# One weight tile per gate: how the gate columns of a projection reach TensorE

## The chip, the cores and the metric

The kernel runs on one core of a Trainium2 chip. The metric is the time of one execution on the device, in microseconds. Before the change three executions took 1739.06, 1737.99 and 1738.39 us; the median is 1738.39 us.

## The reference, cut to what matters

The program is a decoder trunk of two layers over 512 tokens of width 1024. In each layer one projection of the normalised input `u` feeds three attention mixers and three gates:

```
z = u @ w_in                      # 7240 columns; the last 3 * 1024 are the gates
o_a, o_b, o_c = sparse attention, dilated attention, windowed attention with sinks
g = sigmoid(gates.reshape(B, L, 3, 1024))
merged = g[:, :, 0] * (o_a @ w_a) + g[:, :, 1] * (o_b @ w_b) + g[:, :, 2] * (o_c @ w_c)
h = h + merged @ w_o
h = h + relu(rmsnorm(h) @ w_up)^2 @ w_down
```

All of it is float32. The gates of one layer are a product of (512 x 1024) by (1024 x 3072).

## The kernel before, in words

**Products in three parts.** A float32 operand is split into a high part (rounded to the engine's float32r format) and a low part (what is left). `mm3` (lines 285 to 290) multiplies high by high, high by low and low by high, three matmuls into one PSUM tile. The activations `uT` stay split in SBUF for the whole layer. Weights are split as they arrive: `load` (lines 256 to 266) takes a `raw` tile of 128 partitions by 1024 columns, issues the DMAs into it on SP's queue (L261), casts it on ScalarE to `hi` (L264) and subtracts on VectorE to get `lo` (L265). The pool holds 6 `raw` tiles, 5 `hi` tiles and 5 `lo` tiles, and nearly every weight of the program passes through these rings (the MLP's `split`, L925 and L926, takes its `hi` and `lo` tiles from them too). A new tile is cast only when the oldest `hi` tile has been read for the last time.

**A gates chunk.** The 1024 gate columns are cut into eight chunks `f` of 128 columns. `gates` (lines 854 to 869) loads the weights of chunk `f` for all three gates with `load_chunk` (lines 268 to 283). That makes four tiles; tile j holds rows 256j to 256j + 255 of the weight matrix (two blocks of 128 rows, the contraction's `k` = 2j and 2j + 1) for 3 x 128 columns, so it is 768 columns wide and comes by three DMAs of 128 KB. The product of each gate then runs over k = 0..7, 24 matmuls of 512 columns, and so goes through all four tiles; the tiles come free one after another while the third gate is computed. Each gate ends with a tanh on ScalarE (L865) that is stored to DRAM, to be used by `branches` later. `gates` is a generator that yields after k = 3 and after each gate, six times for a chunk.

**What runs beside it.** `build` (from line 1147) draws steps of the gates in turn with steps of the attention mixers, two chunks beside each: chunks 0 and 1 beside `c_attend`, 2 and 3 beside the first `b_attend`, 4 and 5 beside the second, 6 and 7 beside `a_attend`, each time in both layers. Ahead of each of these lies a projection (`c_project`, `b_project`, `a_project`) whose own chunk is four tiles of the same rings. The steps of `topk` (L509, L510, VectorE only) are drawn with both `b_attend`s. The order of instructions on each engine in this part of the program is made when the program is built, by a list scheduler that goes by the order of the drawing and by when operands and buffers are expected to be ready; on the chip each engine runs its list strictly in order.

**Other lines that the prediction names.** L321, L322 and L325 are the rotary embedding of a projection's result on VectorE, L337 the transpose of it on TensorE, L682 the split of keys and queries on VectorE. L381 and L745 are the first steps of a softmax on VectorE, L386 and L750 its exponentials on ScalarE. L406 and L407 split the transposed probabilities, L757 and L561 are those transposes. L849 and L850 split the mixers' outputs for `branches`, whose weights pass through `load` as well.

Of the kernel before, what the change touches and what calls it, by code (L numbers as in the profile page):

```python
# [22 lines left out]
P = 128  # L23
T = 512
NT = 4
D = 1024
NK = 8
# [11 lines left out]
OFF_G = 4168  # L39
# [4 lines left out]
class Trunk:  # L44
# [808 lines left out]

    def gates(self, uT, w, f, sgs):
        nc = self.nc
        wk = self.load_chunk(w, 0, NK, [(OFF_G + i * D + f * P, P) for i in range(3)])
        for i in range(3):
            ps = self.psum([P, T], "g")
            for k in range(NK):
                lhs = tuple(x[:, i * P : (i + 1) * P] for x in wk[k])  # L860
                self.mm3(ps, lhs, (uT["hi"][:, k, :], uT["lo"][:, k, :]), k == 0, k == NK - 1)
                if k == 3:
                    yield
            sg = self.st([P, T], "t")
            nc.scalar.activation(sg, ps, AF.Tanh, scale=0.5)  # L865
            d = self.dr.tile([P, T], F32, name=self.uid("sgd"))
            nc.sync.dma_start(d, sg)
            sgs.append(d)
            yield
# [433 lines left out]
```

## Time and profile before

| | |
|---|---|
| median of 3 executions | 1738.39 us |
| profiled execution, own time | 1737.1 us |
| its span (first to last instruction) | 1735.4 us |
| TensorE (PE) busy | 1688.8 us, 97% |
| weight loads on TensorE (PEld) | 1429.2 us, 82% |
| VectorE (DVE) busy | 1304.6 us, 75% |
| ScalarE (ACT) busy | 919.4 us, 53% |
| mean granted TensorE clock | 0.997 |

How to read it: matmuls are pipelined, and each shows a duration longer than its distance to the next one, so a busy PE can still hide short gaps. Idle time of an engine counts only where something on the chain that ends last waits for it. A row of the chain of waits is a piece of that chain: the engine and line that the end of the program hung on at that time.

### The profile page before, as it was taken

The page shows a single profiled execution, that of the slowest core. Times are in us where ns is not written, and L with a number is a line of the kernel's source. Part 1 is how long each engine was busy: PE and PEld are TensorE (multiplying, and loading weights), DVE is VectorE, ACT ScalarE, POOL GpSimd, SP SyncE. Part 2 cuts the span into 40 slices and gives each one's busy share as a digit, 9 for nine tenths or more (in the row PEclk, how much of TensorE's full clock was granted, in tenths as well). Part 3 has the DMA queues.
Part 4 walks back from the last instruction along what each step waited for, and adds up shares of the span by engine and source line. Part 5 has one row for each costly group of instructions (what it writes and reads, how often), then busy time and mean ns, then how long its engine had stood idle before and what let it go on. Part 6 is the DMA issues. An engine that isn't in the chain of part 4 may idle for free.

```text
span 1735.4 us, 24490 instructions
## 1 busy us (share of the span) xinstructions
PE 1688.8 (97%) x8640; PEld 1429.2 (82%) x8640; DVE 1304.6 (75%) x2643; ACT 919.4 (53%) x1861; POOL 25.7 (1%) x80
## 2 busy tenths in 40 slices
PE   6999999999999999999999999999999999999997
PEld 4879889787789888888887898988778898888886
DVE  7886976968864858685888868597789568585868
ACT  5475655546533645454545855455473255455454
POOL 1100000000000000000000000000000000000000
PEclk9999999999999999999999999999999999999999
DMA  5333334332662142423343253433238423241411
GB/s 166 89 92 114 84 90 109 104 78 83 221 211 91 62 144 85 136 90 105 101 128 73 68 133 87 109 77 98 75 109 275 161 85 110 85 133 61 156 40 72
DMA packets 202908, 190.54 MB, mean 110 GB/s; under 512 B 17824, under 2 KB 159136, under 8 KB 202784
## 3 DMA queue, kind: packets, MB, share of 16 engines
q1 hardware_dynamic: 202784, 188.97, 36.6%
q8 instruction: 68, 1.11, 0.3%
q14 instruction: 56, 0.46, 0.1%
HBM read 167.91 MB, written 18.87 MB: 108 GB/s over the span
## 4 chain that ended last, share of the span: by engine, by line
PE 81%; DVE 12%; ACT 4%; issue 2%; DMA 1%; POOL 0%; SPq 0%; DVEq 0%; POOLq 0%; ACTq 0%
PE psg L288 20%; PE psg L289 20%; PE psg L290 20%; PE psl L289 2%; PE psl L290 2%; PE psl L288 2%; PE pst L337 2%; PE pst L289 1%; PE pst L290 1%; PE pst L288 1%; DVE a L682 1%; DVE lo L265 1%; PE psl L369 1%; PE pst L561 1%; PE psl L370 1%
## 5 line engine op out<-in xcount | busy, mean ns | idle before, releaser
L288 PE MATMUL psg<-uT,hi 128*128 128x512 f32 (+1 forms) x896 | 347.2, 387 | 0.0
L289 PE MATMUL psg<-uT,hi 128*128 128x512 f32 (+1 forms) x896 | 345.9, 386 | 0.0
L290 PE MATMUL psg<-uT,lo 128*128 128x512 f32 (+1 forms) x896 | 344.1, 384 | 0.0
L265 DVE TENSOR_TENSOR lo<-raw,hi 128x768 fp32r<-128x768 f32 (+4 forms) x256 | 262.8, 1031 | 56.3 <-ACT hi L264 54.0
L264 ACT CAST hi<-raw 128x768 fp32r<-128x768 f32 (+4 forms) x256 | 229.6, 900 | 129.8 <-PE psg L289 48.4
L288 PE MATMUL psg<-hi,uT 128*128 128x384 f32 (+2 forms) x624 | 220.9, 355 | 1.4 <-DVE t L322 1.4
L290 PE MATMUL psg<-hi,uT 128*128 128x384 f32 (+2 forms) x624 | 219.0, 352 | 0.6 <-DVE uT L241 0.6
L289 PE MATMUL psg<-lo,uT 128*128 128x384 f32 (+2 forms) x624 | 219.1, 352 | 0.1
L290 PEld LDWEIGHTS psg<-uT,lo 128*128 128x128 f32 x896 | 169.1, 189 | 31.7 <-DVE lo L265 0.9
L288 PEld LDWEIGHTS psg<-uT,hi 128*128 128x128 f32 x896 | 169.2, 189 | 30.2 <-issue 1.5
L289 PEld LDWEIGHTS psg<-uT,hi 128*128 128x128 f32 x896 | 169.2, 189 | 28.8
L925 ACT CAST hi<-raw 128x1024 fp32r<-128x1024 f32 x80 | 84.2, 1052 | 81.4 <-DVE raw L1000 34.6
L288 PEld LDWEIGHTS psg<-hi,uT 128*128 128x128 f32 x624 | 118.3, 190 | 8.4 <-issue 1.6
L289 PEld LDWEIGHTS psg<-lo,uT 128*128 128x128 f32 x624 | 118.1, 189 | 8.2 <-DVE lo L265 1.5
L290 PEld LDWEIGHTS psg<-hi,uT 128*128 128x128 f32 x624 | 118.0, 189 | 7.7 <-DVE uT L241 1.3
L926 DVE TENSOR_TENSOR lo<-raw,hi 128x1024 fp32r<-128x1024 f32 x80 | 96.0, 1218 | 25.4 <-ACT hi L925 25.4
L956 DVE TENSOR_TENSOR a<-t,a 128x512 fp32r<-128x512 f32 (+1 forms) x128 | 78.9, 620 | 46.9 <-ACT a L955 45.3
L288 PE MATMUL psg<-hi,a 128*128 128x512 f32 x288 | 112.5, 390 | 0.0
L290 PE MATMUL psg<-hi,a 128*128 128x512 f32 x288 | 112.2, 389 | 0.0
L289 PE MATMUL psg<-lo,a 128*128 128x512 f32 x288 | 112.0, 389 | 0.0
L964 ACT ACTIVATE t<-psg 128x512 f32<-128x512 f32 x60 | 35.7, 595 | 120.4 <-PE psg L290 120.4
L407 DVE TENSOR_TENSOR a<-pst,a 128x384 fp32r<-128x384 f32 (+1 forms) x100 | 60.5, 622 | 36.8 <-ACT a L406 36.3
(229 smaller groups left out, 3232.0 us busy)
## 6 DMA issues: line engine op xcount, KB each, us to landing
raw<-in_w_in_dram SPq DMA_DIRECT2D x336, 128.0 KB, 2.8
raw<-in_w_up_dram SPq DMA_DIRECT2D x128, 256.0 KB, 3.7
raw<-in_w_down_dram SPq DMA_DIRECT2D x48, 512.0 KB, 4.7
raw<-in_w_in_dram SPq DMA_DIRECT2D x24, 512.0 KB, 3.6
sgd<-t SPq DMA_DIRECT2D x48, 256.0 KB, 2.2
t<-sgd SPq DMA_DIRECT2D x48, 256.0 KB, 4.3
raw<-in_w_o_dram SPq DMA_DIRECT2D x16, 512.0 KB, 4.4
a<-in_w_down_dram SPq DMA_DIRECT2D x16, 512.0 KB, 4.3
```

Source lines behind the costliest of these rows:

```text
L264: nc.scalar.copy(hi[:, :width], raw[:, :width])
L265: nc.vector.tensor_tensor(lo[:, :width], raw[:, :width], f32(hi[:, :width]), op=ALU.subtract)
L288: nc.tensor.matmul(out, lh, rh, start=start, stop=False, **kw)
L289: nc.tensor.matmul(out, lh, rl, start=False, stop=False, **kw)
L290: nc.tensor.matmul(out, ll, rh, start=False, stop=stop, **kw)
L337: self.nc.tensor.transpose(ps[:, i, :], src[:, i * P : (i + 1) * P], self.ident)
L369: nc.tensor.matmul(out, q, k[:, 0, c0 : c0 + n], start=True, stop=False)
L407: self.last_dve = nc.vector.tensor_tensor(pt[:, 1, :n], ps, f32(pt[:, 0, :n]), op=ALU.subtract)
L925: nc.scalar.copy(hi, x)
L926: nc.vector.tensor_tensor(lo, x, f32(hi), op=ALU.subtract)
L956: v.tensor_tensor(lo, x, f32(hi), op=ALU.subtract)
L964: nc.scalar.activation(r, ps, AF.Relu)
```

## The change

A chunk is loaded as three tiles, one for each gate, with all eight blocks of 128 rows side by side: 1024 columns wide, one DMA of 512 KB. The matmul of gate i and block k takes its 128 columns from tile i at place k. The split of a tile is the same `load` as before: cast on ScalarE, subtraction on VectorE. The products, their order and the yields stay.

```
     def gates(self, uT, w, f, sgs):
         nc = self.nc
-        wk = self.load_chunk(w, 0, NK, [(OFF_G + i * D + f * P, P) for i in range(3)])
+        wk = []
+        for i in range(3):
+            c0 = OFF_G + i * D + f * P
+            src = w[:, c0 : c0 + P].rearrange("(k p) n -> p k n", p=P)
+            wk.append(self.load([(lambda raw: raw.rearrange("p (k n) -> p k n", n=P), src)], D))
         for i in range(3):
             ps = self.psum([P, T], "g")
             for k in range(NK):
-                lhs = tuple(x[:, i * P : (i + 1) * P] for x in wk[k])
+                lhs = tuple(x[:, k * P : (k + 1) * P] for x in wk[i])
                 self.mm3(ps, lhs, (uT["hi"][:, k, :], uT["lo"][:, k, :]), k == 0, k == NK - 1)
                 if k == 3:
                     yield
```

## Rows read from the trace of the kernel before

**Rows 1.** The page: busy time by engine; chain that ended last, by engine.
```profile
PE 1688.8 (97%) x8640; PEld 1429.2 (82%) x8640; DVE 1304.6 (75%) x2643; ACT 919.4 (53%) x1861; POOL 25.7 (1%) x80
...
PE 81%; DVE 12%; ACT 4%; issue 2%; DMA 1%; POOL 0%; SPq 0%; DVEq 0%; POOLq 0%; ACTq 0%
```

**Rows 2.** Chain of waits over the whole span, shares by line.
```profile
by line: PE psg L288 20.2%; PE psg L289 20.2%; PE psg L290 20.1%; issue 2.0%; PE psl L289 1.9%; PE psl L290 1.9%; PE psl L288 1.9%; PE pst L337 1.7%; PE pst L289 1.4%; PE pst L290 1.4%; PE pst L288 1.3%; DVE a L682 1.2%; DVE lo L265 1.2%; P
```

**Rows 3.** Waits of TensorE, in total: us, times, longest us.
```profile
PEld psl L369 <- DVE st L381: 6.8, 14, 1.0
...
PEld psg L289 <- DVE lo L265: 1.5, 5, 0.6
...
PEld psg L290 <- DVE lo L265: 0.9, 4, 0.2
...
PE pst L337 <- DVE t L325: 9.2, 14, 1.3
```

**Rows 4.** Groups by shape: count, busy us, mean ns, idle before and releasers.
```profile
L265 DVE TENSOR_TENSOR lo<-raw,hi 128x1024 fp32r<-128x1024 f32 x104 | 126.4, 1220 | 47.4 <-ACT hi L264 46.8
L265 DVE TENSOR_TENSOR lo<-raw,hi 128x768 fp32r<-128x768 f32 x112 | 105.9, 948 | 7.6 <-ACT hi L264 6.1 <-PE psg L290 0.5
L264 ACT CAST hi<-raw 128x1024 fp32r<-128x1024 f32 x104 | 109.3, 1051 | 74.5 <-PE psl L290 28.2 <-DMA raw<-in_w_up_dram 13.6 <-PE psg L289 12.0
L264 ACT CAST hi<-raw 128x768 fp32r<-128x768 f32 x112 | 93.0, 836 | 18.8 <-PE psg L289 8.0 <-PE psg L290 7.4 <-ACT a L672 2.3
```

**Rows 5.** Stretches: length, busy us of each engine (instructions), granted clock, DMA.
```profile
100.00:103.60 3.60, 2.36 (x13) 1.67 (x13) 3.54 (x19) 2.72 (x11) 0.00 (x0) 1.00 0.45 105
103.70:107.10 3.40, 3.40 (x10) 2.61 (x9) 2.16 (x13) 2.85 (x13) 0.00 (x0) 0.51 0.21 77
949.00:956.00 7.00, 5.71 (x33) 4.61 (x32) 6.76 (x24) 3.45 (x13) 0.00 (x0) 1.00 0.32 92
204.00:220.00 16.00, 14.33 (x82) 11.46 (x81) 14.63 (x45) 8.18 (x23) 0.00 (x0) 1.00 0.49 115
309.00:332.00 23.00, 19.73 (x115) 15.15 (x113) 22.47 (x58) 10.07 (x30) 0.00 (x0) 1.00 0.37 109
```

**Rows 6.** VectorE in order of time, 203 to 219: start us, us, instruction.
```profile
204.00 0.94 DVE L265 TENSOR_TENSOR lo<-raw,hi 128x768 fp32r<-128x768 f32 x1
...
206.94 0.95 DVE L265 TENSOR_TENSOR lo<-raw,hi 128x768 fp32r<-128x768 f32 x1
207.80 0.55 DVE L325 TENSOR_TENSOR t<-t,t 128x384 f32<-128x384 f32 x1
...
215.11 0.95 DVE L265 TENSOR_TENSOR lo<-raw,hi 128x768 fp32r<-128x768 f32 x1
```

**Rows 7.** TensorE in order of time, 205 to 214, idle before and releaser.
```profile
208.50 0.52 PE L337 MATMUL pst<-ident,t 128*128 128x128 f32 x3 [0.51 <-DVE t L325]
```

**Rows 8.** VectorE in order of time, 308 to 327.
```profile
309.34 0.94 DVE L265 TENSOR_TENSOR lo<-raw,hi 128x768 fp32r<-128x768 f32 x1
...
322.66 0.95 DVE L265 TENSOR_TENSOR lo<-raw,hi 128x768 fp32r<-128x768 f32 x1
```

**Rows 9.** VectorE in order of time, 96 to 102.5.
```profile
97.72 0.95 DVE L265 TENSOR_TENSOR lo<-raw,hi 128x768 fp32r<-128x768 f32 x1
```

**Rows 10.** VectorE in order of time, 396 to 398.
```profile
396.74 0.96 DVE L265 TENSOR_TENSOR lo<-raw,hi 128x768 fp32r<-128x768 f32 x1
```

**Rows 11.** ScalarE in order of time, 84 to 115, idle before and releaser.
```profile
89.48 0.83 ACT L264 CAST hi<-raw 128x768 fp32r<-128x768 f32 x1 [0.53 <-PE psg L290]
...
114.60 0.84 ACT L264 CAST hi<-raw 128x768 fp32r<-128x768 f32 x1 [0.41 <-PE psg L289]
```

**Rows 12.** ScalarE in order of time, 438 to 453.
```profile
443.51 0.73 ACT L264 CAST hi<-raw 128x640 fp32r<-128x640 f32 x1 [0.47 <-PE psg L289]
...
445.38 0.62 ACT L264 CAST hi<-raw 128x512 fp32r<-128x512 f32 x1 [0.38 <-PE psg L289]
```

**Rows 13.** Tile raw: all its loads, time from issue to landing.
```profile
DMA to landing us min/median/max: 2.0/3.1/10.9
```

## The prediction

> **What bounds the kernel now.** I read the busy times first: TensorE is busy 97% of the span, and the chain that ended last lies on it for 81%, on VectorE for 12%, on ScalarE for 4% [rows 1]. By line that chain is the three matmuls of `mm3`, and among the small entries stands the subtraction of the weight split, L265, with 1.2% of 1735.4 us, some 21 us [rows 2]. So the matmuls set the time, except in stretches where VectorE is late. The edit leaves every matmul as it is. It can move the time in two ways: by what TensorE waits for, and by what the splits cost on VectorE and ScalarE where those engines are the late ones.
>
> The waits of TensorE come next. For gate or projection weights it hardly waits: the two rows on `lo` L265 add to 2.4 us in the whole program [rows 3]. The waits that count are for the rotary embedding (9.2 us on L325) and for the softmax (6.8 us on L381), which run on VectorE [rows 3]. The stretches say where. Where an attention begins, just behind a projection, VectorE has no room: 14.63 of 16 us beside the first `b_attend`, 22.47 of 23 beside the second, 3.54 of 3.6 at `c_attend`, while TensorE is busy for only 14.33, 19.73 and 2.36 us [rows 5]. The splits of the gates stand in these very stretches: from 204.00 to 215.11 there are four of them [rows 6], from 309.34 to 322.66 four more [rows 8], at 97.72 one [rows 9], at 396.74 one [rows 10]. The one at 206.94 runs right ahead of the L325 [rows 6] for which TensorE then stands idle 0.51 us [rows 7]. The question is thus how many gate subtractions lie in these tight stretches afterwards, and how long one is.
>
> **The change, part by part.**
>
> *Instructions.* A chunk has four casts of 836 ns and four subtractions of 948 ns now, and will have three of 1051 and three of 1220 [rows 4]. ScalarE: 4 x 836 - 3 x 1051 = 191 ns less for a chunk, VectorE: 4 x 948 - 3 x 1220 = 132 ns less. Over 16 chunks that is 3.1 us of ScalarE and 2.1 us of VectorE, of which only what lies in the tight stretches counts; it is in the terms below. [...]
>
> *Supply of weights.* The first gate of a chunk now needs all of one tile, where the first matmuls needed a quarter of the rows. With a ring of five `hi` and `lo` tiles and a chunk of four, one slot is spare: the first tile of the next chunk is cast ahead, at 89.48 us for chunk 1, whose second follows at 114.60 [rows 11]. So the first tile of each chunk is ready long before its use, and with the change that tile is the whole first gate. Tiles then come free after each gate and not only in the third one, and two slots are spare. Waits for gate weights therefore stay at nothing; the most to be gained are the 2.4 us above. Should the cover fail, a first gate would wait for cast and subtraction, 1051 + 1220 against 836 + 948 ns: 0.49 us for a chunk, 7.8 us for 16.
>
> *DMA.* 12 issues for a chunk become 3 on SP's queue, with the same bytes in the same runs of 512 B (128 columns). A single load of 512 KB in such runs does not stand in the trace; all landings run from 2.0 to 10.9 us, the median is 3.1 [rows 13]. What hides it: the 768-wide casts name no DMA among those who ended their waits [rows 4], and those beside the gates are held up by TensorE's last read of an older tile (0.53 and 0.41 us, [rows 11]). I take 0. Without that cover a chunk could come 10.9 - 3.1 = 7.8 us late, or, by the shortest landing, 1.1 us early; neither fits the rows. The nine issues saved are worth 0 by the same rows.
>
> *The tight stretches of `b_attend` (four, two in each layer).* Now there are four subtractions in each: the last three of the chunk and the first of the next, 4 x 0.948 = 3.79 us. Afterwards the same four slots hold the second and third gate of the chunk and the first two of the next. The first two stay ahead of the attention. Those of the next chunk are drawn later than the attention's first steps and go only where VectorE seemed to have room. If all four stay, 4 x 1.220 = 4.88 us, +1.09. If one falls out, 3.66, -0.13. If both fall out, 2.44, -1.35. I take the middle, because one subtraction of a later chunk does stand there now (215.11 and 322.66). Four stretches: -0.5 us, bounds -5.4 to +4.4.
>
> *`c_attend` and `a_attend` (two each).* One subtraction of a later chunk stands in each [rows 9, 10], and I leave one there, 272 ns longer: 4 x 0.27 = +1.1 us. It may also fall out: bounds -3.8 (four times 0.95) to +1.1.
>
> *`branches`.* Behind the last chunk, the casts for the first branch weights hold ScalarE for 0.47 and 0.38 us until the third gate has read a tile for the last time [rows 12], and the splits of the outputs stand behind them. With slots free after each gate these two waits go: 0.85 us of ScalarE in each layer. What is late next is the last of the attention itself, so I count 0.5 us of it, 1.0 us for both layers, bounds 0 to 1.7.
>
> *Sum.* -0.5 + 1.1 - 1.0 = -0.4 us. Against the profiled execution's own 1737.1 us (span 1735.4 and 1.7 around it) that is 1736.7. The median of the runs shown, 1738.39, lies 1.3 us above that execution, so the forecast is 1738.0 us: no change. I take 0.2%, 3.5 us, as what a measurement of this kernel can tell from none. The forecast's own range is 1735 to 1741.5.
>
> **Rivals.**
>
> *Faster: the tight stretches lose two splits.* Both subtractions of the next chunk go behind the attention's start, as the drawing order alone would have it, and the first gate, which needs none of the chunk's later tiles, fills TensorE. Then the four `b_attend` stretches give -5.4, `branches` -1.0, and the other four starts come out even: 1738.4 - 6.4 = 1732.0. For it: the later splits are no longer due at once. Against it: 215.11, 322.66 and 97.72 show later chunks' splits already placed inside the attention's start.
>
> *Slower: four longer splits in the same places.* The order of instructions stays, and each subtraction in a tight stretch is 272 ns longer: 16 in the `b_attend`s give +4.4, four at the others +1.1, and `branches` nothing: 1738.4 + 5.5 = 1743.9. It decides from the point where all four of a `b_attend` stay between the projection's last transposes and the second exponentials. For it: VectorE is full there, and the chain of waits runs through L265. Against it: the fourth is due latest.
>
> [...]
>
> *The edit does not do what it says.* The scheduler could keep the late casts, and tiles would come free early for nothing. Then all is as before but for the longer splits, which is the slower case.
>
> **How the numbers follow.** Forecast 0.42, all of it within 0.2% (1734.9 to 1741.9). Faster case 0.32, below 1734.9. Slower case 0.19, above 1741.9. Clock 0.07, half of it above. So faster 0.32, same 0.45 (0.42 + 0.03), slower 0.23. The range leaves out about a tenth at each end: below, the faster case with a part of the other starts' -3.8 (1732.0 - 2 = 1730); above, the slower case (1743.9) and a little of the clock: 1745.
>
> **What would show it.** The group of L265 with 768 columns falls from 112 to 48 and that with 1024 rises from 104 to 152, with 1220 ns each. Step by step: the waits on `lo` L265 stay under 2.4 us; between 204 and 220 three subtractions of 1.22 us stand where four of 0.95 stood; the idle times ahead of the branch casts at 443 and 445 are gone; the clock dips once. The forecast is wrong if the two `b_attend` stretches hold two subtractions (faster) or four (slower), if TensorE's idle time ahead of L337 and L381 moves by more than 3.5 us in all, or if a wait on `hi` or `lo` of a gate appears at the head of a chunk.

## The result, and the profile after

The kernel with one tile per gate takes 1752.36 us (median of 4 runs, 1749.84 to 1753.42) against 1738.19 us (1737.0 to 1739.06) for the kernel before: a ratio of 1.0081, 95% interval [1.0069, 1.0093], 14.2 us slower. The forecast was 1738.0 us, no change. The profiled execution took 1752.46 us, with a span of 1750.8.

The page of the kernel after, busy time by engine and the chain that ended last (for [rows 1]):

```profile
PE 1694.3 (97%) x8640; PEld 1430.4 (82%) x8640; DVE 1303.9 (74%) x2627; ACT 915.8 (52%) x1845; POOL 25.7 (1%) x80
...
PE 78%; DVE 14%; ACT 5%; issue 2%; DMA 1%; POOL 0%; SPq 0%; POOLq 0%; DVEq 0%; ACTq 0%
```

VectorE and ScalarE have less work than before, and still the chain lies on them for three points more (12 + 4% before, 14 + 5% now). So no engine got more instructions (TensorE runs the same 8640 matmuls); TensorE waits more. The groups of the split, by shape (for [rows 4]):

```profile
L265 DVE TENSOR_TENSOR lo<-raw,hi 128x1024 fp32r<-128x1024 f32 x152 | 184.4, 1217 | 56.6 <-ACT hi L264 55.9
...
L265 DVE TENSOR_TENSOR lo<-raw,hi 128x768 fp32r<-128x768 f32 x48 | 45.7, 953 | 12.1 <-ACT hi L264 10.5 <-DMA raw<-in_w_in_dram 0.4
```

What TensorE and its weight loads wait for (total us, times, longest), first the kernel before (other waits than [rows 3]), then the kernel after:

```profile
PEld pst L561 <- DVE a L400: 4.5, 16, 0.5
...
PEld pso L415 <- ACT a L406: 2.2, 11, 0.3
...
PEld pso L289 <- DVE a L407: 1.0, 2, 0.5
```

```profile
PE pst L337 <- DVE t L325: 10.5, 12, 1.4
...
PEld pso L415 <- ACT a L406: 7.6, 23, 0.7
...
PEld pst L561 <- DVE a L400: 7.6, 14, 1.2
...
PEld psl L369 <- DVE st L381: 6.4, 16, 0.8
PEld pso L289 <- DVE a L407: 5.2, 6, 1.8
...
PEld psg L289 <- DVE lo L265: 3.4, 9, 1.1
```

The two waits on which the prediction kept its eye, L325 and L381, hardly moved (9.2 to 10.5 and 6.8 to 6.4). The ones that grew are those for L406, L407 and L400, on which the prediction's sum has no term: the probabilities of `b_attend` and `a_attend`.

**Where it was lost.** TensorE runs the same matmuls in both kernels, so I followed single instructions: the difference of the start of the same instruction (kernel after minus before), at the end of a stretch less that at its beginning. The ends, in layer 1 of the kernel before, are VectorE's L321 at 276.8 us and TensorE's L757 at 334.8 (the start of the second `b_attend`), L757 at 355.8 to L321 at 368.3 (its end), L321 at 387.0 (`a_project`), TensorE's first L561 at 398.2 (the start of `a_attend`) and its last one at 446.4. The table holds layer 1 / layer 2 in us for all kernels run, each from its one profiled execution; a d marks a stretch in which the granted TensorE clock fell in that profile (to 0.50 or 0.51 over 3.4 us where a row here shows it), and the last two columns are the median less that of the kernel before in the same session, and the ratio's interval.

| kernel | 2nd `b_attend`, start | its end | `a_project` | `a_attend`, start | `a_attend` | time | ratio |
|---|---|---|---|---|---|---|---|
| after | 1.42 / 3.03d | 1.65 / 1.50 | 0.76 / 0.77 | 0.89 / 0.89 | 2.30 / 2.28 | +14.2 | [1.0069, 1.0093] |
| e1 chunks 6, 7 | 0 / 0 | 0 / 0 | 0.77 / 0.78 | 0.88 / 0.89 | 2.30 / 2.36 | +5.0 | [1.0019, 1.0043] |
| e2 chunks 4, 5 | 1.49 / 3.02d | 1.54 / 1.60 | 0 / 0.01 | 0.01 / 0 | 0.01 / -0.01 | +7.3 | [1.0029, 1.0053] |
| e9 chunks 0 to 3 | 0.02 / 0.85d | 0 / 0 | 0 / 0 | 0 / 0.01 | 0.03 / 0 | -0.2 | [0.9990, 1.0007] |
| e3 order, end of `b_attend` | 1.43 / 1.46 | 0 / 0 | 0.77 / 0.77 | 0.88 / 0.87 | 2.86d / 2.28 | +10.8 | [1.0049, 1.0073] |
| e4 and last gate late | 1.42 / 1.66 | 0 / 0 | 0.76 / 0.78 | 0.89 / 0.87 | 1.69 / 1.68 | +7.7 | [1.0033, 1.0057] |
| e5 and order of `a_attend` | 1.58 / 3.05d | 0 / 0 | 0.77 / 0.78 | 0.88 / 0.88 | -0.15 / 1.06d | +6.6 | [1.0025, 1.0052] |
| e6 three tiles, by rows | 1.53 / 1.45 | 0 / 0 | 0.77 / 0.77 | 0.83 / 0.86 | 1.77d / 1.50d | +7.4 | [1.0031, 1.0056] |
| e7 four tiles, by gates | 1.70d / 1.69d | 0 / 0 | 0 / 0 | 0.48 / 0.49 | 3.23 / 3.28 | +9.4 | [1.0042, 1.0068] |
| e8 small DMAs | 1.44 / 1.44 | 1.59 / 1.61 | 0.77 / 0.77 | 0.89 / 0.88 | 2.39d / 2.34 | +12.5 | [1.0058, 1.0086] |
| e10 e2, chunk 5 held | 0.97 / 1.00 | 1.52 / 1.59 | 0 / 0 | 0 / 0.01 | -0.03 / 0 | +5.2 | [1.0017, 1.0040] |
| e11 e5, chunk 5 held | 1.02 / 0.99 | 0 / 0 | 0.77 / 0.78 | 0.90 / 0.89 | -0.13 / 1.14d | +6.3 | [1.0023, 1.0051] |

Without the clock a layer of the kernel after loses 1.43 + 1.6 + 0.77 + 0.89 + 2.3 = 7.0 us, two layers 14.0 us, where the medians differ by 14.2. The first `b_attend` and the MLP lose less than 0.1 us, `c_attend` 0.15 in layer 2; in layer 1 it gains 1.2, because the fall of the clock at 103.7 us [rows 5] is in the kernel before alone (1.00 in the same 3.4 us of the kernel after). `branches` loses 0.3 and 1.0 behind a fall of the clock (0.50 at 452.5 us and 0.51 at 1312.6), but in layer 2 e9 and e10, whose last chunks are the old ones, lose 1.1 and 1.0 there too. The columns say better where the time goes than how much: summed they come to up to 3.0 us more than the medians differ (most for e1, 8.0 against 5.0), in part because the profiled execution of the kernel before was one of its fastest (1737.1 us).

The five terms are of two kinds: longer subtractions in places where VectorE is the limit (third column, and a part of the first and fourth), and orders of instructions that came out otherwise (second and fifth, and a part of the first).

**Longer subtractions.** Stretches of the kernel after: length, busy us of PE, PEld, DVE, ACT, POOL (instructions), clock, DMA share, GB/s (for [rows 5]). The last two show the clock behind two gaps:

```profile
204.00:220.00 16.00, 14.16 (x81) 11.48 (x80) 15.69 (x44) 8.71 (x22) 0.00 (x0) 1.00 0.39 97
309.00:332.00 23.00, 18.59 (x107) 13.88 (x106) 22.59 (x53) 11.51 (x29) 0.00 (x0) 1.00 0.38 115
...
452.50:455.90 3.40, 3.40 (x12) 3.06 (x11) 2.98 (x6) 2.89 (x7) 0.00 (x0) 0.50 0.00 0
1189.80:1193.20 3.40, 3.40 (x11) 2.92 (x11) 3.40 (x10) 1.67 (x5) 0.00 (x0) 0.50 0.42 103
```

The subtractions of the split alone (L265), in the same form with VectorE only, before and then after:

```profile
204.00:220.00 16.00, 3.78 (x4) 1.00 0.49 115
...
306.00:336.00 30.00, 5.67 (x6) 1.00 0.30 86
...
368.00:392.00 24.00, 2.84 (x3) 1.00 0.26 67
```

```profile
204.00:220.00 16.00, 5.42 (x5) 1.00 0.39 97
309.00:332.00 23.00, 5.76 (x5) 1.00 0.38 115
...
306.00:336.00 30.00, 7.22 (x6) 1.00 0.36 106
...
368.00:392.00 24.00, 3.55 (x3) 1.00 0.16 49
```

The number of subtractions did not fall with the number of tiles in a chunk: six before and six after between 306 and 336 us, three and three in `a_project`. That fits the rings, which hold five tiles whatever is in them, so that as many tiles as before can be split ahead, each a third larger; a ring of another length was not tried. In the second `b_attend` that is 7.22 - 5.67 = 1.55 us more, and 1.42 us were lost; in `a_project` 0.71 more, 0.76 lost. The first `b_attend` took 5.42 - 3.78 = 1.64 more (one is cut off by the stretch's end) and lost nothing: VectorE had 16 - 14.63 = 1.37 us free there [rows 5] and has 0.31 left, while in the second it had only 23 - 22.47 = 0.53.

In the second `b_attend` the sum of 1.55 is not the whole account, for e6 (below) loses as much with five subtractions, 6.04 us in place of 5.67 up to the same L407 (L265 alone in e6):

```profile
306.00:337.00 31.00, 6.04 (x5) 1.00 0.30 86
```

What the kernel after and e6 share is found a step earlier, at the fifth L745, the softmax's first step. VectorE there, before, after and in e6:

```profile
327.92 0.41 DVE L745 CUSTOM_DVE_ANT_0 a<-psl,m_b 128x256 f32<-128x256 f32 x1
...
328.92 0.68 DVE L407 TENSOR_TENSOR a<-pst,a 128x512 fp32r<-128x512 f32 x1
```

```profile
325.95 1.20 DVE L265 TENSOR_TENSOR lo<-raw,hi 128x1024 fp32r<-128x1024 f32 x1
...
327.74 0.68 DVE L407 TENSOR_TENSOR a<-pst,a 128x512 fp32r<-128x512 f32 x1
...
328.94 0.40 DVE L745 CUSTOM_DVE_ANT_0 a<-psl,m_b 128x256 f32<-128x256 f32 x1
```

```profile
328.13 0.68 DVE L407 TENSOR_TENSOR a<-pst,a 128x512 fp32r<-128x512 f32 x1
...
329.33 0.40 DVE L745 CUSTOM_DVE_ANT_0 a<-psl,m_b 128x256 f32<-128x256 f32 x1
```

Counted from the last L322 of `b_project` (306.79, 306.27 and 306.65), this L745 starts after 21.13 us before and after 22.67 and 22.68 in the other two, 1.54 later (and as much in layer 2). Ahead of it stand four subtractions in all three, 3.77 us before and 4.82 in the others, which is 1.05 more; and the L407 of 0.68 us that stood behind it stands ahead of it. So about 1.0 of the loss is the length of subtractions and about 0.5 an order that turned. That is read from the traces; no run sets this order back.

**An order that turned on VectorE.** VectorE in order of time at the end of the second `b_attend`, before and after (start us, us, instruction, idle before and releaser):

```profile
356.92 0.69 DVE L407 TENSOR_TENSOR a<-pst,a 128x512 fp32r<-128x512 f32 x1 [0.87 <-ACT a L406]
359.93 0.18 DVE L797 TENSOR_TENSOR s<-bst,bst 128x16 f32<-128x16 f32 x1 [2.33 <-DMA bst<-bt]
```

```profile
356.50 1.22 DVE L265 TENSOR_TENSOR lo<-raw,hi 128x1024 fp32r<-128x1024 f32 x1
359.75 0.17 DVE L797 TENSOR_TENSOR s<-bst,bst 128x16 f32<-128x16 f32 x1 [2.02 <-DMA bst<-bt]
...
360.13 0.68 DVE L407 TENSOR_TENSOR a<-pst,a 128x512 fp32r<-128x512 f32 x1
```

Before, the last split of probabilities (L407) stands ahead of L797 of `b_merge`, which waits for a DMA. After, a weight subtraction of 1.22 us stands where L407 stood, and L407 came behind L797; it had nothing to wait for but its place in the queue: ScalarE's cast L406 for it ran from 356.71 us for 0.59, and L407 starts 2.83 us after the end of that. TensorE in the kernel after stands still for it, with nothing else to do:

```profile
360.87 0.27 PE L289 MATMUL pso<-a,a 128*64 128x128 f32 x1 [1.45 <-DVE a L407]
```

**An order that turned on TensorE.** Beside `a_attend` the gate matmuls are what TensorE does while the softmax is not ready. At the end of it, the last transposes of probabilities (L561), before and after:

```profile
441.92 0.63 PE L561 MATMUL pst<-ident,a 128*128 128x128 f32 x4
442.31 0.47 PE L289 MATMUL psg<-uT,hi 128*128 128x512 f32 x1
...
443.31 0.43 PE L561 MATMUL pst<-ident,a 128*128 128x128 f32 x2
443.50 0.48 PE L290 MATMUL psg<-uT,lo 128*128 128x512 f32 x1
```

```profile
447.57 0.39 PE L290 MATMUL psg<-uT,lo 128*128 128x512 f32 x1
448.60 0.63 PE L561 MATMUL pst<-ident,a 128*128 128x128 f32 x4 [0.64 <-DVE a L400]
450.21 0.44 PE L561 MATMUL pst<-ident,a 128*128 128x128 f32 x2 [0.99 <-DVE a L400]
451.11 0.44 PE L415 MATMUL pso<-a,a 128*128 128x384 f32 x1 [0.46 <-ACT a L406]
```

Before, gate matmuls stand behind each of these transposes and TensorE has no idle time from 441.92 to 445.58 us; after, the gates are used up at 447.57 and it waits three times. Counting how many of the 60 transposes of a layer stand ahead of each half gate of the last two chunks (from the fourth half gate on): 6, 12, 12, 18, 27, 33, 36, 48, 48 before, 2, 6, 12, 18, 18, 27, 33, 36, 48 after. The matmuls that were the filling were spent earlier.

### The profile page after: what moved, and what is told of

Same layout as the page of the kernel before. It is cut to its first block, busy times and chain, and to the rows that moved or that the text cites. A ratio compares the mean times of both kernels' runs of the same rounds, so it can differ in the third digit from the quotient of the medians.

```text
span 1750.8 us, 24125 instructions
## 1 busy us (share of the span) xinstructions
PE 1694.3 (97%) x8640; PEld 1430.4 (82%) x8640; DVE 1303.9 (74%) x2627; ACT 915.8 (52%) x1845; POOL 25.7 (1%) x80
## 4 chain that ended last, share of the span: by engine, by line
PE 78%; DVE 14%; ACT 5%; issue 2%; DMA 1%; POOL 0%; SPq 0%; POOLq 0%; DVEq 0%; ACTq 0%
PE psg L288 19%; PE psg L289 19%; PE psg L290 19%; PE psl L289 2%; PE psl L290 2%; PE psl L288 2%; PE pst L337 2%; DVE a L682 2%; DVE lo L265 1%; PE pst L289 1%; PE pst L290 1%; PE pst L288 1%; DVE m L509 1%; PE psl L369 1%; ACT hi L264 1%
## 5 line engine op out<-in xcount | busy, mean ns | idle before, releaser
L265 DVE TENSOR_TENSOR lo<-raw,hi 128x1024 fp32r<-128x1024 f32 (+3 forms) x240 | 260.8, 1090 | 73.0 <-ACT hi L264 70.6
L264 ACT CAST hi<-raw 128x1024 fp32r<-128x1024 f32 (+3 forms) x240 | 227.0, 948 | 143.5 <-PE psg L289 67.0
L959 ACT CAST a<-t 128x512 fp32r<-128x512 f32 (+1 forms) x128 | 70.1, 567 | 32.4 <-DVE t L950 30.8
```

The source lines that it names most:

```text
L264: nc.scalar.copy(hi[:, :width], raw[:, :width])
L265: nc.vector.tensor_tensor(lo[:, :width], raw[:, :width], f32(hi[:, :width]), op=ALU.subtract)
L959: nc.scalar.copy(hi, x)
```

## The experiments

Parts of the change come first, then orders set back by hand, then the two properties of the new tiles, one at a time. The code is cut to what matters.

**e1, the last two chunks alone.** `load_one_per_gate` stands for the new loading in the change.

```
+        if f >= 6:
+            wk = load_one_per_gate
+        else:
             wk = self.load_chunk(w, 0, NK, [(OFF_G + i * D + f * P, P) for i in range(3)])
```

> The new loading for chunks 6 and 7 alone (beside a_attend), the old for 0 to 5. Theory O (the loss is a matter of order: a list scheduler that sees the splits elsewhere runs the gates' matmuls ahead of a_attend, 12 to 14 of them, and leaves its tail without any): the loss from a_project on comes back in full, about +4 us in each layer with the clock dips, so 1738 + 7 to 9 = 1745 to 1747 us, with no gate matmul behind the last eight transposes. Theory W (each 1024-wide split holds its engine 272 ns longer): two chunks of eight carry a quarter of the loss, 1738 + 3.5 = 1741.5.

1743.57 us against 1738.59, between the two expectations in time. The trace decides where: only `a_project` and `a_attend` lose, 3.95 us in layer 1 and 4.03 in layer 2, as in the whole change. That is 8.0 us where the medians differ by 5.0; the two profiled executions are 7.4 apart, that of the kernel before 1.5 us under its median and that of e1 0.9 above.

**e2, chunks 4 and 5 alone** (`if f in (4, 5):`).

> The new loading for chunks 4 and 5 alone (beside the second b_attend). Theory O: the order of VectorE is turned round at the end of that b_attend (the last probability split behind a step that waits for a DMA), 1.6 us of idle TensorE in each layer, and 1.4 us more at its start: +3 us in each layer and a clock dip in one, 1738 + 6 to 8 = 1744 to 1746 us. Theory W: a quarter of the loss, 1741.5.

1745.85 us. The losses at the start and the end of the second `b_attend` are those of the whole change, and there are no others.

**e9, chunks 0 to 3 alone** (`if f < 4:`).

> Chunks 0 to 3 alone (beside `c_attend` and the first `b_attend`) come as one tile a gate, chunks 4 to 7 as before. Place theory (the loss lies in three places only: the start of the second `b_attend`, its end, and `a_attend`, all of which take the tiles of chunks 4 to 7): 1737 to 1740 us, ratio 1.000, and with the two kernels that had the new loading at chunks 4 and 5 alone (+7.1 us) and at 6 and 7 alone (+5.4 us) the three losses add to about the 14 us of the whole change. Rival (a cost that every chunk pays, such as the longer subtraction wherever VectorE is full, or the large DMA): half of the chunks, so half of the 14 us, 1745 us.

1738.55 us against 1738.72: no change, though half of all chunks come as large tiles. The three parts give -0.2 + 7.3 + 5.0 = 12.1 us; with intervals of some 2 us each that is consistent with the whole. So there is no cost that every chunk pays; what counts is where its tiles fall.

**e8, small DMAs.** One tile per gate, by four DMAs of 128 KB each.

```
-            src = w[:, c0 : c0 + P].rearrange("(k p) n -> p k n", p=P)
-            wk.append(self.load([(lambda raw: ..., src)], D))
+            parts = [(blocks 2j and 2j + 1 of raw, the 256 rows of w) for j in range(4)]
+            wk.append(self.load(parts, D))
```

> The changed kernel with four DMAs of 128 KB into a tile and not one of 512 KB; the order on the other engines is that of the changed kernel. If the loads' size mattered (later landing of the whole tile) this would give some of the 14 us back; every theory of order or width expects no change, 1752 us.

1751.29 us, and the table's row is that of the kernel after: the size of the DMA is not the cause.

**e3, the turned order on VectorE set back.** The whole change, with L797 held behind the last L407.

```
-        v.tensor_tensor(nM, nm0, nm1, op=ALU.min)
+        with self.tc.issue_after(self.last_split.ins): v.tensor_tensor(nM, nm0, nm1, op=ALU.min)
```

> The changed kernel with one edge more: the first step of b_merge that waits for a DMA stands behind the last probability split on VectorE. Theory O: the idle 1.45 us ahead of the value product at 361 us and its like in layer two go, 1752.4 - 3.2 = 1749 us. Theory W: the splits are as long as before, no change, 1752.4.

1749.42 us, 2.9 less than the change, and the second column is zero. VectorE of this kernel:

```profile
357.38 1.22 DVE L265 TENSOR_TENSOR lo<-raw,hi 128x1024 fp32r<-128x1024 f32 x1
358.52 0.68 DVE L407 TENSOR_TENSOR a<-pst,a 128x512 fp32r<-128x512 f32 x1
360.63 0.18 DVE L797 TENSOR_TENSOR s<-bst,bst 128x16 f32<-128x16 f32 x1 [1.43 <-DMA bst<-bt]
```

The long subtraction is still there and costs nothing; the 1.6 us were the wait of L797 ahead of L407. Shown.

**e4, filling kept for the end.** e3, and the third gate of chunk 7 held behind late transposes.

```
+                    if f == NK - 1 and i == 2:
+                        held.enter_context(self.tc.issue_after(self.pes[-13 if k < 4 else -7].ins))
```

> As the run before, and the last gate of chunk 7 is held behind transposes of the last a_attend unit, so that 24 gate matmuls remain for the tail. Theory O: the tail's idle 3 us in each layer go, and the two clock dips that follow it: 1749 - 2 x 2.8 = 1743 us or a little less. Theory W: no change but for the edge, 1749 to 1752.

1746.33 us, 3 us above the expectation: `a_attend` still loses 1.69 in a layer. The rows of TensorE show why: the end is filled better, and a gap has opened where the held matmuls were.

```profile
439.29 0.44 PE L561 MATMUL pst<-ident,a 128*128 128x128 f32 x2 [1.06 <-DVE a L400]
...
446.83 0.63 PE L561 MATMUL pst<-ident,a 128*128 128x128 f32 x4 [0.56 <-DVE a L400]
448.13 0.44 PE L561 MATMUL pst<-ident,a 128*128 128x128 f32 x2 [0.68 <-DVE a L400]
```

**e5, the order of `a_attend` set back as a whole.** e3, and the half gates of chunks 6 and 7, from the fourth on, held behind as many transposes as before, by the counts above.

```
+                    n = {3: 6, 4: 12, 5: 12, 6: 18, 7: 27, 8: 33, 9: 36, 10: 48, 11: 48}.get(6 * f + 2 * i + k // 4 - 36, 0)
+                    if n:
+                        held.enter_context(self.tc.issue_after(self.pes[n - 1].ins))
```

> The changed kernel with the edge at the end of b_attend (as e3_order_b_tail) and with each half of a gate in chunks 6 and 7 held behind that transpose of a_attend behind which it stood before the change (for instance the fifth half behind 12 transposes, where the change let it run behind 6). Theory O: what e4_hold_last_gate only moved (3.4 us in each a_attend) goes: 1746.3 - 2 x 2.5 to 3.4 = 1739.5 to 1741.5 us. Rival P (a_attend's own softmax is late, because splits of later weights stand in front of it on ScalarE and VectorE, whatever TensorE's order is): the idle time moves again, 1746 us.

1745.46 us, near the rival's number; but the trace bears out the order: in layer 1 `a_attend` loses nothing any more (-0.15 for 2.30). TensorE of this kernel at the same transposes has no idle time:

```profile
444.58 0.63 PE L561 MATMUL pst<-ident,a 128*128 128x128 f32 x4
...
445.77 0.44 PE L561 MATMUL pst<-ident,a 128*128 128x128 f32 x2
```

The expectation was off because it took all that is left for small; the start of the second `b_attend`, `a_project` and the start of `a_attend` keep 3.2 us in a layer. In layer 2, where the clock falls in this stretch (in e11, which sets the same order there, the granted clock is 0.74 from 1259 to 1265 us), 1.06 are lost, so the order's worth is shown in layer 1 alone.

**e6 and e7, the two properties apart.** e6 has three tiles of 1024 columns as the change, but filled by rows, so that every gate needs all of them to the end. e7 has four tiles of 768 columns as before, but filled gate after gate, so that they come free early.

```
e6:  tile = (3 * k + i) // 8       e7:  tile = (8 * i + k) // 6
```

> Three tiles of 1024 columns, but filled by rows as before the change: eight of the 24 blocks each, in the order (k, gate), so that all tiles come free in the third gate. Width alone, without the early release. Theory W, sharpened (longer splits in the tight stretches): the b_attend start costs 4 x 0.27 = 1.1 us in each and a_attend's order (half 4 behind 6 transposes and not 12) costs 3.4 in each layer: 1738.6 + 2 x (1.1 + 3.4) = 1747 us. Theory R (it is the early release that lets a fifth split into the start of b_attend): 4 splits of 1.22 there and not 5, 1738.6 + 2 x 3.4 = 1745 us.

> Four tiles of 768 columns as before, but filled gate by gate (six blocks each), so that they come free from the first gate on. Early release without width. Theory R: five splits of 0.95 at the start of the second b_attend, +1 us in each layer, and a_attend's order as after the change (half 4 behind 6 transposes, half 7 behind 18): 1738.6 + 2 x (1 + 3.4) = 1747 us. Theory W: 1738.6 and only what the order in a_attend brings, 1745 us or less.

1746.27 and 1748.23 us: neither property alone is the cause, and each has its columns in the table. The size gives the loss in `a_project` (0.77 with 1024 columns, 0 with 768, whoever fills them). At the start of the second `b_attend` both lose. e6 loses 1.53 and 1.45 with no fall of the clock (1.00 from 306 to 337 us), as shown above. e7 loses 1.70 and 1.69, but the clock falls in this stretch in both layers (0.93 over the 23 us from 309 in layer 1), and by the trace it has seven subtractions (6.61 us) up to the L407 up to which the kernel before has six (5.67). What of its loss is the clock and what the seventh subtraction, this pair of runs cannot tell.

`a_attend` loses in both, 1.5 to 1.8 by rows and 3.2 by gates. The turned order on VectorE comes with neither alone.

**e10, the same subtractions a step later.** e2, with VectorE's subtractions for chunk 5 held behind the first three L407 of the second `b_attend`.

```
+                self.hold = self.splits[self.first_split + i] if f == 5 else None
```

> Chunks 4 and 5 alone as one tile a gate, as in the kernel that took 1745.85 us, but VectorE's subtractions for the three tiles of chunk 5 are held behind the first, second and third L407 (the low part of the transposed probabilities) of the second `b_attend`, each one step later than the scheduler put it. Crowding theory (each of these subtractions stood right ahead of an L407 or an L745 for which TensorE waits): the 1.4 us at the start of the second `b_attend` go in each layer, and with them the gap that was followed by the half clock: 1741 to 1743.5 us. Rival (it is the sum of VectorE's work in the stretch, six subtractions of 1.2 us where six of 0.95 stood, wherever they stand): no change, 1745 to 1747 us.

1743.9 us, by 2 us below e2. The loss at the start is 0.97 and 1.00 in place of 1.49 and 3.02; 1.5 of the latter were a fall of the clock that this profile does not have (from 1182 to 1190 us it is 0.79 in e2 and 1.00 in e10). Another 0.2 us is lost just behind the end of that column, in the same group of transposes, so that 1.2 of 1.45 us stays. The sum of subtractions, L265 alone in the columns used above, is that of e2 (7.24 us):

```profile
306.00:336.00 30.00, 7.24 (x6) 1.00 0.33 93
```

So the crowding theory, which expected all to go, is refuted as the main cause. The step of the three subtractions is worth about 0.25 us. The fifth L745 of this kernel (its line 749) bears out the order told above: it starts 21.69 us after the L322, 0.56 later than before, with less subtraction ahead of it (3.62 us for 3.77) and the same L407 in front.

**e11, all three orders set.** e5 with e10's edit.

> The new loading everywhere, with all three orders set: VectorE's L797 of `b_merge` behind the last L407, the half gates of chunks 6 and 7 behind the transposes of `a_attend` where they stood before (these two gave 1745.46 us), and in addition the subtractions of chunk 5 held behind the first three L407 of the second `b_attend`. If the three places are the whole loss: 1739.5 to 1743 us. If the second `b_attend` loses by the sum of VectorE's work and not by the order: 1745 us.

1745.06 us. The terms of its row, a fall of the clock in layer 2 among them, add to 6.4 us, and 6.7 with the 0.2 us behind the first column, where 6.3 were measured: 1.2, 0.77 and 0.9 in each layer are left, the places of the longer subtractions. No version of the new loading was faster than the kernel before.

## Why the prediction was wrong, point by point

**Instructions: right.** The groups moved as said, 152 and 48 of them with 1217 and 953 ns, and VectorE's splits fell by 126.4 + 105.9 - 184.4 - 45.7 = 2.2 us (2.1 worked out); all of VectorE's work fell by 0.7. Three large subtractions took less of the engine than four small ones, 3 x 1217 against 4 x 948 ns for a chunk, and the program took 14.2 us more: the engine's busy time did not tell the program's.

**Supply and DMA: right in size.** Waits on `lo` L265 rose from 2.4 to 3.9 us (3.4 and a row of 0.5 for TensorE itself), where they were to stay under 2.4, and e8 shows that the size of the transfers is worth little: 1751.29 us for 1752.36.

**The tight stretches: the step that failed.** "I take the middle": three subtractions in each `b_attend` start in place of four, -0.5 us. The step counted the tiles of a chunk. But in the second `b_attend` four stayed ahead of the fifth L745 and six up to the fourth L407, as many as before, each some 0.26 us longer, and TensorE lost 1.42 us there, not -0.13. The step's upper bound of +1.09, four longer ones, holds the part that is length (1.05). It does not hold the L407 that came ahead of the L745, because the step took the order as given. For the first `b_attend` the step feared too much in its upper bound: five stood there, and nothing was lost, where 1.37 us of VectorE had been free.

**`a_project`: missing.** It was not in the sum at all. It holds three subtractions on VectorE ahead of the rotary embedding, and lost 3 x 0.25 us in each layer.

**`c_attend` and `a_attend`, one subtraction of 0.27 each: mis-sized.** `c_attend` lost 0.15 in layer 2. The start of `a_attend` lost 0.89; 0.48 with tiles of 768 columns, so the length of one subtraction is only about 0.4 of it. What makes the rest was not settled; the trace of the kernel after shows VectorE idle for 0.63 us ahead of an L350 at 396.27 us, for a cast (L349) that waits 1.61 us for transposes on TensorE, where the kernel before has no such wait.

**The order elsewhere: about half.** All terms of the sum, and the slower rival in its very words ("the order of instructions stays"), took the order of the attention's own instructions for given. It changed in two places, apart from the L407 at the start of the second `b_attend`, and these cost 2 x (1.6 + 2.3) = 7.8 of the 14 us by the table; setting them back gave 2.9 (e3) and 4.0 (e5) by the medians. Nothing in the trace of before could give those numbers, but it did hold the exposure: L407 next to an instruction that waits 2.33 us for a DMA, and an `a_attend` whose end is filled with gate matmuls to the last. Why the scheduler turned just these was not tried; e6 and e7 only show that each of size and early release moves `a_attend`, and that neither alone turns VectorE.

**`branches`: right in the wait, wrong in its worth.** The idle time ahead of the casts at 443 and 445 us [rows 12] is gone: the casts at the end of `a_attend` in the kernel after show none.

```profile
438.54 0.71 ACT L264 CAST hi<-raw 128x640 fp32r<-128x640 f32 x1
...
448.12 0.60 ACT L264 CAST hi<-raw 128x512 fp32r<-128x512 f32 x1
```

It gave nothing back: in e1, whose mean granted clock is that of the kernel before (0.997), the way from the last transpose past `branches` to the next transposes (530.8 us in the kernel before) is as long as before, to 0.02 us. Splits that nobody waited for became earlier.

**The slower rival** had the sign, and its mechanism, longer splits with the order kept, is some 2 x (1.05 + 0.77 + 0.4) = 4.4 of the 14 us. That this is near its price of 5.5 is in part luck, for the places are others: not the first `b_attend` and not `c_attend`, but `a_project`, which it did not name. It stood at 0.19 because the fourth split seemed due late.

**The clock and the signs.** The fall at `c_attend`, one in the trace of before, did not come (1.2 us gained in layer 1), and three others came (granted clock 0.50 at 452.5 us, 0.50 at 1189.8, 0.51 at 1312.6) where the forecast expected one in all. The chance of 0.07 for the clock and its part in the range were the author's estimate: no run shows what makes the clock fall. What the runs showed is the loss with one fall, 3.03 us at the start of the second `b_attend` in layer 2 where e8, without it, lost 1.44. Of the signs of being wrong, four subtractions in a `b_attend` stretch (and more) came true; the idle time ahead of L337 and L381 moved by only +1.3 and -0.4 us, because TensorE waited elsewhere.

## What to carry to other kernels

Where a list scheduler orders the program, changing the size of a tile changes which instructions stand next to each other on every engine, far from the edit; look in the profile for places that only their order protects (a short instruction ahead of one that waits for a DMA, filling matmuls that last just to the end) and price their loss. Larger tiles through a ring with a fixed number of slots need not mean fewer instructions in a stretch: here six of 0.95 us became six of 1.20. Count them up to the same later instruction in both traces, since a stretch fixed in time cuts one off or takes one in. And compare the free time of the busy engine in each stretch with what is added: where 1.37 us were free the longer instructions cost nothing, where 0.53 were free four of them cost about 1.0 us.

## What the runs showed of the hardware

TensorE's clock fell in one profile and not in another, and in one layer and not in the other, behind the same instructions. The start of the second `b_attend` in layer 2, first the kernel after and then e8, which runs the same instructions there:

```profile
1180.00:1193.00 13.00, 10.10 (x59) 7.66 (x60) 13.00 (x33) 6.67 (x17) 0.00 (x0) 0.88 0.44 122
```

```profile
1180.00:1193.00 13.00, 10.11 (x69) 7.61 (x68) 13.00 (x34) 6.92 (x17) 0.00 (x0) 1.00 0.44 115
```

Over these 13 us TensorE is busy for 10.10 us in the one and 10.11 in the other, yet the granted clock is 0.88 in one (0.50 for 3.4 us of it, the row at 1189.80 above) and 1.00 in the other. The loss with the fall is 3.03 - 1.44 = 1.6 us larger. The same is seen within one execution, that of the kernel after. In the 9.8 us from 1180.00, ahead of the fall, TensorE is busy for 6.90 us and its last waits are 0.88, 0.37, 0.69 and 0.57 us. In the same stretch of layer 1, the 9.8 us from 321.38, it is busy for 6.92 us with waits of 0.87, 0.37, 0.69 and 0.57 us, and the clock stays at 1.00 up to 336. What makes it fall is not shown by these runs. Apart from one fall near 43 us, which the kernels before and after both have (0.53 and 0.50 over 3.4 us), and from the last microseconds, the kernel before has one and the kernel after three; the mean granted clock of the profiled executions is from 0.995 (after, e7) to 0.998 (e10). So the columns of the table, with the d marks, and not the last microseconds of a median, tell the mechanisms apart.
